# Seven products in the first pass of each MLP, the turned order in every pass, and pads between SBUF tiles

## The chip, the cores and the metric

The kernel runs on one core of a Trainium2 chip. The metric is the device time of one execution in microseconds (us); the median of three runs counts. TensorE (PE) multiplies matrices out of SBUF into the eight banks of PSUM, and its weight loads (PEld) run beside it. VectorE (DVE) and ScalarE (ACT) do element by element work, GpSimd (POOL) a few fills, and SyncE (SP) issues the DMAs that bring weights from HBM.

## The reference, cut to what matters

Two decoder layers over 256 positions with a width of 2048 in float32. The first mixes with a gated short convolution, the second with latent attention; each ends with an MLP, and every sub-layer with a layer norm of the residual.

```python
def sq_relu_mlp(x, w1, w2):
    return jnp.square(jax.nn.relu(x @ w1)) @ w2      # 2048 -> 8192 -> 2048

def reference(...):
    for layer in range(DEPTH):                        # DEPTH = 2
        ...
        h = layer_norm(ALPHA * h + mix, ln_g[layer, 0], ln_b[layer, 0])
        h = layer_norm(ALPHA * h + sq_relu_mlp(h, mlp_w1[layer], mlp_w2[layer]),
                       ln_g[layer, 1], ln_b[layer, 1])
    return h
```

## The kernel before

**Split operands.** The matmuls take operands rounded from float32 (type fp32r). Every operand is split into a high part (a cast on ScalarE, L121) and a low part (a subtraction on VectorE, L122), and a product is high x high + high x low + low x high.

**The weight stream.** All weights pass through one list, `stream`, in blocks of 128 x 1024. `take` hands out the next block and calls `prepare` for blocks up to five ahead: SyncE loads a raw block (five buffers, tag raw), ScalarE and VectorE split it into tiles hi and lo (eight buffers each). An entry of the list with two blocks becomes a pair (below). The order in which each engine finally runs its instructions is made by a scheduler from the order in which they are written, the priorities being that order; so work that waits for nothing may stand earlier on VectorE or ScalarE than it does in the text.

**The MLP** (`mlp`, called twice) walks over the 8192 hidden columns in NQ = 8 passes of QC = 8 blocks of 128. A pass has two halves:

- *Up.* Eight units, one for each hidden block. In pass 0 they are done by `mm_wide` on the input before its norm (258 columns: 256 positions and two columns for the norm's gain and offset), with x in the tiles of tags a1 and a2. From pass 1 on they are done by `products`: for each of 16 blocks k one matmul `high` with 512 columns (high and low part of x beside each other, L199) and one `low` with 256 (L203), 256 matmuls in a pass, x (`xhl`) in tag b. With `turned` set, unit 0 does low before high at k = TURNED = 2 once; before, this is so in pass 1 alone. Units put their sums into banks 0 and 1 in turn. `hidden` evacuates a unit, squares it and splits it into h (tag c).
- *Down.* h times the rows of w2, into four output blocks n of 512 columns for two halves t of the positions. `dot` does the three matmuls of a split product, 512 columns each (L283 to L285). Here h (128 columns) is loaded as the stationary operand, and the weights stream.

`down` does one output block in the plain way: 8 x 2 products, 48 matmuls. The passes in FAST (1 to 6) use Strassen-Winograd products instead: two blocks of h, two halves of the positions and two output blocks form a 2 x 2 by 2 x 2 product of blocks, which takes seven `dot`s in place of eight (`fast_products`, FACTORS). For this `prepare` builds from a pair of raw blocks the sums T1 to T4 (L154, L157, L160), and `hidden` builds S1 to S4 from h (L662 to L665) into `forms` (tag a2). The seven sums stay in seven banks and are added to `acc` (tag a1) or to `sums` by `keep` (L588; in pass 1 four of them are copied, L586). `fold`, in the last pass, adds `sums` into `acc`. In `down_pairs` the first two output blocks take four such units (84 matmuls); the last two follow MIXED = "ppsp": three quarters plain, the third quarter by seven products.

In pass 0 and pass 7 all four output blocks are plain: 192 matmuls. In pass 0 `put` copies a finished block to `acc` on ScalarE (L573) and then writes two calls of `normal` (L466 to L471), which compute the normed x for pass 1. In the second MLP passes 1 to 4 also add the turned residual (`extra`). In the first MLP, `begin` prepares the next norm (L397), written in the last pass.

**SBUF.** Pools are laid one behind another, and in a pool each tag gets its place when it is first used, as large as its largest tile: before, in pool act, xres, a1, a2, b, c, then S, Q, mu0 and ab; after act come raws, whl (hi, lo), tmp, small, and then the pool of the MLP (sums, fp, sf, t4).

Of the kernel before, what the change touches and what calls it, by code (L numbers as in the profile page):

```python
# [16 lines left out]
P = 128  # L17
W = 256 + 2
T = 256
# [16 lines left out]
BW = D // NB  # L36
FAST = range(1, NQ - 1)
MIXED = "ppsp"
FIRST = (0, 1, 2, 4, 6, 8, 12, 16)
HEAD = 4  # L40
GROUP = 3
# [10 lines left out]
def trunk(ctx: ExitStack, tc: tile.TileContext, xT, vecs, w_first, w_in, w_out, w_kv, w_q, w_uk, w_uv,  # L52
# [22 lines left out]
    def mlp_stream(l):  # L75
        out = []
        for q in range(NQ):
            out += halves(w1[l, q * QC:(q + 1) * QC])
            if q not in FAST:
                out += halves(w2[l, q])  # L80
                continue
            out += [(w2f[l, q, j, 0], w2f[l, q, j, 1]) for j in range(QC // 2)]
            for j, kind in enumerate(MIXED):
                if kind == "s":
                    out.append((w2g[l, q, j, 0], w2g[l, q, j, 1]))
                else:
                    out += halves(w2[l, q, 3, j]) + halves(w2[l, q, 2, j])
        return out
# [96 lines left out]
    def psum(name, bank=None):  # L185

        bank = Banks.next() if bank is None else bank
        return (pmm if bank < 4 else Banks.more).tile([P, 512], F32, tag=f"mm{bank}", name=name)
# [89 lines left out]
            yield ps  # L278


    def dot(ps, w, x, first, last):

        nc.tensor.matmul(ps, x[0], w[0], start=first, stop=False)  # L283
        nc.tensor.matmul(ps, x[0], w[1], start=False, stop=False)  # L284
        nc.tensor.matmul(ps, x[1], w[0], start=False, stop=last)  # L285

    def held(x, t):

        return [x[:, o + t * P:o + (t + 1) * P] for o in (0, T)]
# [2 lines left out]

        return [v[:, 4 * kk:4 * kk + 4, :].rearrange("p a c -> p (a c)") for v in w]

    def down(x, put, n):

        ps = [psum("ps_d") for _ in range(2)]
        for j in range(len(x) // 2):
            w, = take(1)
            for kk in range(2):  # L300
                k = 2 * j + kk
                for t in range(2):
                    dot(ps[t], wide_rows(w, kk), held(x[k], t), k == 0, k == len(x) - 1)
        for t in range(2):
            put(n, t, ps[t])
# [11 lines left out]
                put(n, t, ps)  # L317

    OWN, KEPT = ("1", "5", "7", "6"), (2, 3, 4, 5, 6, 7, 0)


    FACTORS = (("3", "S4", "22"), ("1", "11", "11"), ("5", "S1", "T1"), ("7", "S3", "T3"),
# [175 lines left out]
    banks = Banks.open("first")  # L498


    xres = act.tile([P, NC, T], F32, tag="xres", name="xres")
# [51 lines left out]
    def mlp(idx, ln, blocks, fast, begin=None, extra=None):  # L553
# [17 lines left out]
        def put(n, t, ps):  # L571
            if q == 0:
                nc.scalar.copy(block(n, t), ps)  # L573
                for _ in range(2):
# [6 lines left out]
        def keep(p, g, ps):  # L581

            at = sums[:, OWN.index(p), g, :] if p in OWN else \
                block(*{"2": (2 * g, 0), "3": (2 * g + 1, 0), "4": (2 * g, 1), "22": (2 * g + 1, 1)}[p])
            if q == 1 and p in OWN:
                nc.scalar.copy(at, ps)  # L586
            else:
                nc.vector.tensor_tensor(at, at, ps, ALU.add)  # L588

        def down_pairs(h, forms):  # L590

            n = QC // 2
            ps = {p: psum(f"ps_f{p}", bank) for (p, _, _), bank in zip(FACTORS, KEPT)}
            for j in range(n):
                fast_products(ps, h, forms, j, ps if j == 0 else (), ps if j == n - 1 else ())
            for p in ps:
                keep(p, 0, ps[p])
            ps = {p: psum("ps_d", bank) for p, bank in zip(("22", "3", "2", "4"), (1, *KEPT))}
# [32 lines left out]
        for q in range(NQ):  # L631
            ht = act.tile([P, QC, 2 * T], F32R, tag="c", name=f"h{idx}_{q}")
            h = [ht[:, k, :] for k in range(QC)]
            forms = None
# [4 lines left out]
            def pair_tile(m):  # L639

                if m % 2 == 0:
                    pool = (act, "ab") if m % 4 else (fast, "fp")
                    t = pool[0].tile([P, 2 * T], F32, tag=pool[1], name="fp")
                    pair.append(t.rearrange("p (i t) -> p i t", i=2))
                return pair[-1]

            def hidden(m, ps, evac, *func):
                both = pair_tile(m) if forms is not None else None
                f = both[:, m % 2, :] if forms is not None else tmp.tile([P, T], F32, tag="fh", name="fh", bufs=3)
# [4 lines left out]
                if forms is None:  # L654
                    put_split(h[m], f)
                elif m % 2:
                    at = ht[:, m - 1:m + 1, :]
                    split(at[:, :, :T], at[:, :, T:], both)
                    (a11, a21), (a12, a22) = ((both[:, i, :P], both[:, i, P:]) for i in range(2))
                    sf = fast.tile([P, 4, P], F32, tag="sf", name="sf")  # L660
                    s1, s2, s3, s4 = (sf[:, i, :] for i in range(4))
                    nc.vector.tensor_tensor(s1, a21, a22, ALU.add)  # L662
                    nc.vector.tensor_tensor(s3, a21, a11, ALU.subtract)
                    nc.vector.tensor_tensor(s2, s1, a11, ALU.subtract)
                    nc.vector.tensor_tensor(s4, a12, s2, ALU.subtract)  # L665
                    split(forms[:, m // 2, 0, :], forms[:, m // 2, 1, :], sf.rearrange("p i c -> p (i c)"))

            if q == 0:
                for m in range(QC):
                    if m < GROUP:  # L670
                        if m == 0:
                            ws = ln.ws if ln.ws else group_of(GROUP)
                            if not ln.ws:
                                mm_wide(ws, ln.xd)
                            ln.finish()
                        ps = ws[m][1]
                    else:
                        ws = [(take(), psum("ps_w"))]
                        mm_wide(ws, ln.xd)
                        ps = ws[0][1]  # L680
                    hidden(m, ps, ln.weighted, AF.Relu)
                    if m > 0:
                        normal()
                if begin:
                    begin(range(1))
                acc = act.tile([P, 2, D], F32, tag="a1", name=f"acc{idx}")
            else:
                folds = fold()
                for m, ps in enumerate(products(QC, xhl, TURNED if q == 1 else None, (0, 1))):
                    hidden(m, ps, whole)  # L690
                    if q == NQ - 1:
                        next(folds)
                        if begin:
                            begin(range(max(2 * m, 1), 2 * m + 2))

            if q == NQ - 1:
                blocks(block, put, h)
                return
            if q in FAST:
                down_pairs(h, forms)  # L700
            else:
                for n in range(NB):
                    down(h, put, n)

    def to_wide(block, put, h):

# [408 lines left out]
```

## Time and profile before

| what | value |
|---|---|
| three runs | 2034.58, 2035.73, 2036.16 us; median 2035.73 |
| profiled execution | 2035.76 us |
| its span, first to last instruction | 2034.0 us |
| granted TensorE clock | 1.000 over the whole span |
| VectorE busy | 1686.9 us, 83% |
| ScalarE busy | 1198.7 us, 59% |
| read from HBM | 381.25 MB, 188 GB/s over the span |
| splits of plain blocks (L121, L122) | 710 of each, 1050 and 1220 ns |
| plain down products (ps_d, L283 to L285) | 556 of each line, 391 ns busy |
| up products of passes 1 to 7 (ps_u) | 1792 high, 396 ns; 1792 low, 280 ns |

A matmul's busy time runs from the first column in to the last result out, so that of one overlaps that of the next; what it costs in a row of matmuls is the step from its start to the next one's. Stretches are given in us from the start of the span: the first MLP's pass 0 begins at about 364 with the up units and at 411 with the down products, its pass 1 at 454.8; in the second MLP pass 0's down products begin at 1371.3 and pass 1 at 1414.9.

### The profile page before, as it was taken

How to read it: one execution, taken by the hardware profiler on the slowest of the kernel's cores; microseconds unless marked ns; L12 is line 12 of the kernel's file. 1: busy time of each engine (PE TensorE's matmuls, PEld its weight loads, DVE VectorE, ACT ScalarE, POOL GpSimd, SP SyncE). 2: the span in 40 equal slices, each digit the busy share in tenths (PEclk: the TensorE clock that was granted, in tenths of full speed). 3: DMA queues.
4: the chain of work that ended last, by engine and by line, in shares of the span. 5: the costliest groups of instructions: out<-in, count | busy, mean ns of one | idle time of the engine just before them, and what ended most of it. 6: DMA issues, size and time to landing. Idle time of an engine off the chain costs nothing.

```text
span 2034.0 us, 30032 instructions
## 1 busy us (share of the span) xinstructions
PE 2025.4 (100%) x11204; PEld 1756.3 (86%) x11204; DVE 1686.9 (83%) x2571; ACT 1198.7 (59%) x1829; POOL 2.3 (0%) x21
## 2 busy tenths in 40 slices
PE   9999999999999999999999999999999999999998
PEld 8888888988888888888889998898888888888886
DVE  7667677788898988989888988776889898898986
ACT  6444445676666565655656655566666656566561
POOL 0000000000000000000000000000000000000000
PEclk9999999999999999999999999999999999999999
DMA  8666666564746557465754534656474655746573
GB/s 309 200 188 187 188 193 189 177 196 127 265 147 216 187 177 250 150 222 165 254 171 160 180 118 145 187 179 194 131 244 145 227 193 161 255 150 214 181 237 121
DMA packets 106850, 385.31 MB, mean 189 GB/s; under 512 B 11856, under 2 KB 12752, under 8 KB 106448
## 3 DMA queue, kind: packets, MB, share of 16 engines
q1 hardware_dynamic: 106560, 383.27, 58.6%
q8 instruction: 88, 1.44, 0.3%
q14 instruction: 58, 0.48, 0.1%
q10 hardware_dynamic: 144, 0.13, 0.0%
HBM read 381.25 MB, written 2.10 MB: 188 GB/s over the span
## 4 chain that ended last, share of the span: by engine, by line
PE 93%; DVE 4%; DMA 1%; issue 1%; ACT 1%; DVEq 0%; ACTq 0%
PE ps_u L199 20%; PE ps_l L199 13%; PE ps_u L203 10%; PE ps_l L203 7%; PE ps_d L283 6%; PE ps_d L285 6%; PE ps_d L284 6%; PE ps_f L283 3%; PE ps_f L285 3%; PE ps_f L284 3%; PE ps_w L233 2%; PE ps_w L231 2%; PE ps_w L232 2%; DMA raw<-in_w_dram 1%; DVE lo L122 1%; PE ps_g L233 1%
## 5 line engine op out<-in xcount | busy, mean ns | idle before, releaser
L122 DVE TENSOR_TENSOR lo<-raw,hi 128x1024 fp32r<-128x1024 f32 x710 | 857.4, 1220 | 225.1 <-ACT hi L121 153.8
L121 ACT CAST hi<-raw 128x1024 fp32r<-128x1024 f32 x710 | 741.6, 1050 | 396.8 <-DMA raw<-in_w_dram 117.1
L199 PE MATMUL ps_u<-xhl,hi 128*128 128x512 f32 x1792 | 629.6, 396 | 1.9 <-DVE sums L588 1.9
L203 PE MATMUL ps_u<-xhl,lo 128*128 128x256 f32 x1792 | 502.0, 280 | 0.0
L199 PEld LDWEIGHTS ps_u<-xhl,hi 128*128 128x128 f32 x1792 | 336.1, 188 | 83.7 <-ACT hi L121 3.0
L203 PEld LDWEIGHTS ps_u<-xhl,lo 128*128 128x128 f32 x1792 | 338.4, 189 | 0.6
L199 PE MATMUL ps_l<-xhl_a,hi 128*128 128x512 f32 x704 | 244.1, 393 | 0.0
L283 PE MATMUL ps_d<-hi,h 128*128 128x512 f32 x556 | 217.5, 391 | 0.2 <-DVE sums L588 0.2
L285 PE MATMUL ps_d<-hi,h 128*128 128x512 f32 x556 | 216.6, 390 | 0.0
L284 PE MATMUL ps_d<-lo,h 128*128 128x512 f32 x556 | 216.6, 390 | 0.0
L203 PE MATMUL ps_l<-xhl_a,lo 128*128 128x256 f32 x704 | 195.4, 279 | 0.0
L199 PEld LDWEIGHTS ps_l<-xhl_a,hi 128*128 128x128 f32 x704 | 132.1, 188 | 29.8
L203 PEld LDWEIGHTS ps_l<-xhl_a,lo 128*128 128x128 f32 x704 | 131.9, 188 | 0.2
L121 ACT CAST hi_t<-raw_t 128x1024 fp32r<-128x1024 f32 x60 | 63.0, 1050 | 108.8 <-DVE raw_t L154 93.3
L283 PEld LDWEIGHTS ps_d<-hi,h 128*128 128x128 f32 x556 | 104.4, 188 | 22.6 <-DVE sums L588 0.7
L285 PEld LDWEIGHTS ps_d<-hi,h 128*128 128x128 f32 x556 | 104.4, 188 | 22.1
L284 PEld LDWEIGHTS ps_d<-lo,h 128*128 128x128 f32 x556 | 104.4, 188 | 21.7
L652 ACT ACTIVATE fp<-fp 128x256 f32<-128x256 f32 x96 | 40.0, 417 | 81.5 <-DVE fp L338 80.7
L199 PE MATMUL ps_l<-z,hi 128*128 128x512 f32 x240 | 82.4, 391 | 0.0
L154 DVE TENSOR_TENSOR raw_t<-raw,raw 128x1024 f32<-128x1024 f32 x60 | 73.1, 1219 | 7.4 <-DMA raw<-in_w2f_dram 7.3
L122 DVE TENSOR_TENSOR lo_t<-raw_t,hi_t 128x1024 fp32r<-128x1024 f32 x60 | 73.2, 1220 | 1.3
L233 PE MATMUL ps_w<-xd,hi 128*128 128x258 f32 x256 | 72.9, 285 | 0.0
(270 smaller groups left out, 3359.9 us busy)
## 6 DMA issues: line engine op xcount, KB each, us to landing
raw<-in_w_dram SPq DMA_DIRECT2D x392, 512.0 KB, 4.5
raw<-in_w2f_dram SPq DMA_DIRECT2D x96, 512.0 KB, 3.7
raw<-in_w_in_dram SPq DMA_DIRECT2D x88, 512.0 KB, 4.3
raw<-in_w_out_dram SPq DMA_DIRECT2D x32, 512.0 KB, 4.2
raw<-in_w_o_dram SPq DMA_DIRECT2D x32, 512.0 KB, 4.0
raw<-in_w2g_dram SPq DMA_DIRECT2D x24, 512.0 KB, 5.0
raw<-in_w_kv_dram SPq DMA_DIRECT2D x10, 512.0 KB, 3.6
raw<-in_w_q_dram SPq DMA_DIRECT2D x8, 512.0 KB, 4.2
```

The costliest lines, as they stand in the source:

```text
L121: nc.scalar.copy(hi, src)
L122: nc.vector.tensor_tensor(lo, src, hi.bitcast(F32), ALU.subtract)
L154: nc.vector.tensor_tensor(t.rearrange(two, a=2), b12.unsqueeze(1).to_broadcast([P, 2, BW]), r1.rearrange(two, a=2), ALU.subtract)
L199: nc.tensor.matmul(ps, w[blk // 8][0][:, blk % 8, :], x, start=first, stop=False)
L203: nc.tensor.matmul(ps[:, :T], w[blk // 8][1][:, blk % 8, :], x[:, :T], start=False, stop=last)
L231: nc.tensor.matmul(ps[:, :W], hi, x[k][:, :W], start=k == 0, stop=False)
L232: nc.tensor.matmul(ps[:, :W], lo, x[k][:, :W], start=False, stop=False)
L233: nc.tensor.matmul(ps[:, :W], hi, x[k][:, W:], start=False, stop=k == NC - 1)
L283: nc.tensor.matmul(ps, x[0], w[0], start=first, stop=False)
L284: nc.tensor.matmul(ps, x[0], w[1], start=False, stop=False)
L285: nc.tensor.matmul(ps, x[1], w[0], start=False, stop=last)
L652: nc.scalar.activation(f, f, AF.Relu)
```

## The change

1. **Pads.** xres and the tags c, b, a1 and a2 get their places at the start, with tiles pad0 to pad2 between them and a last one in the pool small, and the tiles that matmuls read (h, xhl, forms, hi, lo, t4) then all begin at one place modulo 512 bytes. The scratch for POOL's DMAs is halved to 2048 bytes.
2. **Seven products in pass 0.** Its output blocks 2 and 3 are done first, plain; blocks 0 and 1 follow by `first_pair`, with the raw blocks as pairs. h of two blocks is kept together in float32 in `sums[:, 0:2]` and split two blocks at a time; the sums S1 to S4 of all four pairs are written behind the last up unit (`form`), when tag a2 is free. All seven results are copied by ScalarE. One block of `acc` is cleared by POOL, and `put` writes three calls of `normal`. In pass 1 the first pair's results are now all added by VectorE.
3. **Banks and order.** In the second pair the four own sums go to banks 0, 5, 6, 7 (before 5, 6, 7, 0), and the other four are added as soon as their block is done.
4. **The turn** stands in every pass from 1 to 7, and one product of the second pair (EVEN) does its middle matmul in two halves of 256 columns.

```diff
+EVEN = (QC - 1, "22")
...
+    xres = act.tile([P, NC, T], F32, tag="xres", name="xres")
+    for tag, columns in (("c", 4096), ("b", 8256), ("pad0", 64), ("a1", 4128), ("pad1", 96), ("a2", 4128), ("pad2", 96)):
+        act.tile([P, columns], F32, tag=tag, name=f"at_{tag}")
+    small.tile([P, 32], F32, tag="pad", name="at_pad", bufs=1)
...
-            if q not in FAST:
+            if q == NQ - 1:
                 out += halves(w2[l, q])
                 continue
+            if q == 0:
+                out += halves(w2[l, q, 2:])
             out += [(w2f[l, q, j, 0], w2f[l, q, j, 1]) for j in range(QC // 2)]
-            for j, kind in enumerate(MIXED):
+            for j, kind in enumerate(MIXED if q else ""):
...
-    def dot(ps, w, x, first, last):
+    def dot(ps, w, x, first, last, two=False):
         nc.tensor.matmul(ps, x[0], w[0], start=first, stop=False)
-        nc.tensor.matmul(ps, x[0], w[1], start=False, stop=False)
+        for at in (slice(0, T), slice(T, 2 * T)) if two else (slice(None),):
+            nc.tensor.matmul(ps[:, at], x[0], w[1][:, at], start=False, stop=False)
         nc.tensor.matmul(ps, x[1], w[0], start=False, stop=last)
...
-            if q == 1 and p in OWN:
+            if q == 0 or q == g == 1 and p in OWN:
                 nc.scalar.copy(at, ps)
...
-                        ps.update({p: psum(f"ps_f{p}", bank) for p, bank in zip(OWN, KEPT[3:])})
+                        ps.update({p: psum(f"ps_f{p}", bank) for p, bank in zip(OWN, OWN_BANKS)})
...
-                            dot(ps[p], wide_rows(w, kk), held(h[k], t), k == 0, k == QC - 1)
+                            dot(ps[p], wide_rows(w, kk), held(h[k], t), k == 0, k == QC - 1, (k, p) == EVEN)
+                    if j == n - 1:
+                        for _, p in two:
+                            keep(p, 1, ps[p])
...
-            for p in ("3", "2", "4", "22"):
-                keep(p, 1, ps[p])
...
+            def form(j):
+                (a11, a21), (a12, a22) = ((pair[j][:, i, :P], pair[j][:, i, P:]) for i in range(2))
+                sf = fast.tile([P, 4, P], F32, tag="sf", name="sf")
+                s1, s2, s3, s4 = (sf[:, i, :] for i in range(4))
+                nc.vector.tensor_tensor(s1, a21, a22, ALU.add)
+                nc.vector.tensor_tensor(s3, a21, a11, ALU.subtract)
+                nc.vector.tensor_tensor(s2, s1, a11, ALU.subtract)
+                nc.vector.tensor_tensor(s4, a12, s2, ALU.subtract)
+                split(forms[:, j, 0, :], forms[:, j, 1, :], sf.rearrange("p i c -> p (i c)"))
...
                 acc = act.tile([P, 2, D], F32, tag="a1", name=f"acc{idx}")
+                forms = act.tile([P, QC // 2, 2, 4 * P], F32R, tag="a2", name=f"forms{idx}_{q}")
+                nc.gpsimd.memset(block(1, 1), 0.0)
+                for j in range(QC // 2):
+                    form(j)
...
-                for m, ps in enumerate(products(QC, xhl, TURNED if q == 1 else None, (0, 1))):
+                for m, ps in enumerate(products(QC, xhl, TURNED, (0, 1))):
...
-            if q in FAST:
-                down_pairs(h, forms)
+            if q == 0:
+                down(h, put, 2, (2, 3))
+                down(h, put, 3, (1, 7))
+                first_pair(h, forms, (0, 2, 3, 4, 5, 6, 7))
             else:
-                for n in range(NB):
-                    down(h, put, n)
+                first_pair(h, forms, KEPT)
+                second_pair(h, forms)
...
-    nc = _bacc.Bacc("TRN2", target_bir_lowering=False, num_devices=1, dynamic_dma_scratch_size=4096)
+    nc = _bacc.Bacc("TRN2", target_bir_lowering=False, num_devices=1, dynamic_dma_scratch_size=2048)
```

`first_pair` and `second_pair` are the two halves of `down_pairs`.

More of the change, by code (lines that the diff above doesn't have):

```diff
@@ L293, in wide_rows, with down @@
         return [v[:, 4 * kk:4 * kk + 4, :].rearrange("p a c -> p (a c)") for v in w]
-    def down(x, put, n):
-        ps = [psum("ps_d") for _ in range(2)]
+    def down(x, put, n, banks=(None, None)):
+        ps = [psum("ps_d", bank) for bank in banks]
         for j in range(len(x) // 2):
@@ L573, in put @@
                 nc.scalar.copy(block(n, t), ps)
-                for _ in range(2):
+                for _ in range(3):
                     normal()
@@ L588, in keep, with first_pair @@
                 nc.vector.tensor_tensor(at, at, ps, ALU.add)
-        def down_pairs(h, forms):
+        def first_pair(h, forms, banks):
             n = QC // 2
-            ps = {p: psum(f"ps_f{p}", bank) for (p, _, _), bank in zip(FACTORS, KEPT)}
+            ps = {p: psum(f"ps_f{p}", bank) for (p, _, _), bank in zip(FACTORS, banks)}
             for j in range(n):
@@ L597, in down_pairs, with second_pair @@
                 keep(p, 0, ps[p])
+        def second_pair(h, forms):
+            n = QC // 2
             ps = {p: psum("ps_d", bank) for p, bank in zip(("22", "3", "2", "4"), (1, *KEPT))}
@@ L633, in mlp @@
             h = [ht[:, k, :] for k in range(QC)]
-            forms = None
+            firsts, forms = sums[:, 0:2].rearrange("p i g c -> p (i g) c"), None
             if q in FAST:
@@ L641, in pair_tile @@
                 if m % 2 == 0:
-                    pool = (act, "ab") if m % 4 else (fast, "fp")
-                    t = pool[0].tile([P, 2 * T], F32, tag=pool[1], name="fp")
+                    if q == 0:
+                        t = firsts[:, m // 2]
+                    else:
+                        pool = (act, "ab") if m % 4 else (fast, "fp")
+                        t = pool[0].tile([P, 2 * T], F32, tag=pool[1], name="fp")
                     pair.append(t.rearrange("p (i t) -> p i t", i=2))
                 return pair[-1]
+            def form(j):
[7 more added lines that the diff above has]
+                split(forms[:, j, 0, :], forms[:, j, 1, :], sf.rearrange("p i c -> p (i c)"))
             def hidden(m, ps, evac, *func):
-                both = pair_tile(m) if forms is not None else None
-                f = both[:, m % 2, :] if forms is not None else tmp.tile([P, T], F32, tag="fh", name="fh", bufs=3)
+                both = pair_tile(m) if q < NQ - 1 else None
+                f = both[:, m % 2, :] if both is not None else tmp.tile([P, T], F32, tag="fh", name="fh", bufs=3)
                 evac(ps, f, *func)
@@ L653, in hidden @@
                 nc.scalar.activation(f, f, AF.Square)
-                if forms is None:
+                if both is None:
                     put_split(h[m], f)
@@ L658, in hidden @@
                     split(at[:, :, :T], at[:, :, T:], both)
[L659 to L666, printed above, removed]
+                    if q:
+                        form(m // 2)
             if q == 0:
```

3 lines of the change are left out of this document (2 added, 1 removed).

## The prediction

> **What bounds the kernel now.** I read the page first, then the busy time by stretch, then single matmuls in the timeline, then the waits, and last VectorE's own timeline around the first pass of each MLP. The profiled execution took 2035.76 us with a span of 2034.0; the runs shown have a median of 2035.73, so the sum below is made against 2035.76 and stands for the median too. A change of this kernel is told from none at about 0.2%, 4.1 us.
>
> ```profile
> PE 2025.4 (100%) x11204; PEld 1756.3 (86%) x11204; DVE 1686.9 (83%) x2571; ACT 1198.7 (59%) x1829; POOL 2.3 (0%) x21
> ```
>
> PE is never idle, so time goes down only by fewer matmuls or by a shorter step from one start to the next. Its busy share can't show that step; counts over stretches can.
>
> ```profile
> 411.10:454.80 43.70, 43.70 (x194) 36.15 (x193) 35.90 (x67) 31.93 (x50) 0.00 (x0) 1.00 0.63 198
> 454.80:499.20 44.40, 44.40 (x258) 39.13 (x257) 33.68 (x51) 27.82 (x46) 0.00 (x0) 1.00 0.46 134
> 499.20:518.70 19.50, 19.50 (x87) 15.81 (x86) 18.07 (x24) 13.02 (x19) 0.00 (x0) 1.00 0.57 190
> 539.90:585.20 45.30, 45.30 (x258) 39.29 (x258) 38.79 (x58) 27.73 (x45) 0.00 (x0) 1.00 0.54 171
> 1371.30:1414.90 43.60, 43.60 (x195) 36.08 (x194) 31.10 (x51) 31.88 (x49) 0.00 (x0) 1.00 0.66 197
> ```
>
> Columns: stretch, length, busy time of PE, PEld, DVE, ACT and POOL with counts (a few at the edges belong to neighbours), clock, DMA. The first and last are pass 0's 192 plain down matmuls: 43.60/192 = 227.1 ns each. The third is the 84 matmuls of one seven-product pair: 19.5/84 = 232.1 ns, though all have 512 columns. The second and fourth are the same 256 up matmuls, 0.9 us apart. The timeline shows why (start, length): the first three lines are a slow pass, the last three a quick one.
>
> ```profile
> 550.17 0.40 PE L199 MATMUL ps_u<-xhl,hi 128*128 128x512 f32 x1
> 550.41 0.28 PE L203 MATMUL ps_u<-xhl,lo 128*128 128x256 f32 x1
> 550.53 0.40 PE L199 MATMUL ps_u<-xhl,hi 128*128 128x512 f32 x1
> ...
> 460.02 0.39 PE L199 MATMUL ps_u<-xhl,hi 128*128 128x512 f32 x1
> 460.25 0.28 PE L203 MATMUL ps_u<-xhl,lo 128*128 128x256 f32 x1
> 460.37 0.39 PE L199 MATMUL ps_u<-xhl,hi 128*128 128x512 f32 x1
> ```
>
> A slow pair takes 0.36 here (353.3 ns over the pass: wide steps of 233, 241 and 236 in turn), a quick pair 0.35 (230 + 117 = 347). Over a whole pass that is 176.6 against 173.4 ns a matmul, 0.82 us in 256. Of the 14 up passes nine are slow: all from pass 2 on in the first MLP; 2, 5 and 7 in the second. The state is chosen at the entry and then holds.
>
> **Fewer products.** Each first pass has 96 plain matmuls left (21.8 us) and 84 in place of 96. At 227.1 ns these take 19.1: 2.7 saved per MLP, 5.4 in two (2.3 and 4.7 at 232.1).
>
> **The pads.** Offsets follow from the tile sizes: a1 and a2 need 16,512 bytes, 128 over a multiple of 512, b 33,024, 256 over; the small pool 896. With the weights at 0 modulo 512, h and a1 lie at 0, forms (a2) at 128, xhl (b) at 256, T4 at 384. After, all are at 0. The row nearest: plain down matmuls, both operands at 0, step 227.1; the seven products alternate stationary operands at 0 and 128, and step 232.1, slowest just after a switch (241) and 227 between two of one h block. I take the gap for the price of switching. The 12 quick passes have 84 + 21 such matmuls: 12 x 105 x 5.0 ns = 6.3 us. Bounds: 0 and, with every switch also delaying its neighbour in the mixed pair, 7.
>
> The Trainium skill says otherwise: in "TensorE: Matmul & The Clock Gate", section "Back-to-back issue gap", a warm step is columns/2.4 plus 2.5 ns, 216 for 512, with no term for an address. The trace's 227.1 and 232.1 agree with neither the figure nor the missing term; by that rule the pads are worth 0, and the time would be that of the second rival.
>
> **The turn in every pass.** Both pass 1 entries, which have it already, come out quick; the others enter as chance has it. I let all nine slow passes become quick: 9 x 0.82 = 7.4. The alike stream ps_l from oT (416 matmuls at 176.4, in tag b) should profit from the pads: 416 x 3.0 ns = 1.2. Together 8.6. Bounds: 10.4 lost (below) to 9.3 gained. No faster state is expected: uniform streams with one offset step 227 (512 columns) and 120 (256, ps_q at 1126 us), together the quick pair's 347. The added turns cost some 20 ns each and the split EVEN matmul 2 x 120 - 227 = 13 ns, twelve times each: 0.4.
>
> **The waits on old sums.** In the second MLP passes 2 to 5 lose time at their end:
>
> ```profile
> PE ps_u L199 <- DVE sums L588: 1.9, 3, 1.0
> PE ps_d L283 <- DVE sums L588: 0.2, 1, 0.2
> ```
>
> Step by step in the timeline these cost 0.15 + 0.34 + 0.40 + 0.87 + 1.11 = 2.9 with the weight load behind them. The next up product needs bank 0, which the fourth addition ("6") frees; after, the first ("1") does, three steps of 0.6 = 1.8 us earlier, more than the longest wait. Late next is bank 1, wanted 5.5 us later, whose "22" is now added first, before the last block ends. I take 2.5.
>
> **VectorE in the first pass** is the price. A plain tile costs it one 128x1024 subtraction, 1.14 us from start to start (two in 2.35 at 1448.38). A pair of raw blocks costs 4 of those and three of 128x512 at 0.6: 6.4 in place of 2.3. Four: 16.3 more. The sums S1 to S4 add 4 x (4 x 0.2 + 0.6) = 5.6, all after the up products, since a2 is still held. So 21.9 more per MLP. DMAs stay: 8 raw blocks of 512 KB before and after.
>
> What hides it? VectorE's timeline:
>
> ```profile
> 435.33 1.21 DVE L122 TENSOR_TENSOR lo<-raw,hi 128x1024 fp32r<-128x1024 f32 x1
> 436.46 1.08 DVE L397 SCALAR_TENSOR_TENSOR xres<-xres,mu 128x256 f32<-128x256 f32 x3
> ...
> 442.53 1.23 DVE L122 TENSOR_TENSOR lo<-raw,hi 128x1024 fp32r<-128x1024 f32 x1 [1.49 <-ACT hi L121]
> ```
>
> ```profile
> 1390.79 0.41 DVE L471 TENSOR_TENSOR xhl<-xres,xhl 128x256 fp32r<-128x256 f32 x1
> 1391.96 1.22 DVE L122 TENSOR_TENSOR lo<-raw,hi 128x1024 fp32r<-128x1024 f32 x1 [0.75 <-ACT hi L121]
> ```
>
> It works without a pause until 441.0 and 1391.2, that is 30.0 and 19.9 us after the down products start; from then on it keeps seven weight tiles ahead of PE (counted: subtractions ended less tiles used) and idles. In the second MLP it has by then tiles 1 to 14; after, 8 of these are plain and the last six (6.8 us) turn into unit 0 (6.4), with 5.6 of sums added: unit 0 at 25, units 1 to 3 at 31.4, 37.8 and 44.2. PE needs a unit's last operand (T4) 18 matmuls, 4.1 us, after it begins it: 25.9 for unit 0, then 4.8 apart. Late: 0.7 + 1.6 + 1.6, and 0.4 for the first tile of pass 1: 4.3. In the first MLP ten replaced tiles (11.4) lie before 441.0: unit 0 and 5.0 of unit 1 at 35.6, unit 1 at 37.0 for 30.7; then 1.6, 1.6 and 0.4: 9.9. There 5.4 us are next-norm rows (L397) that nobody needs before pass 7; behind the units, 4.5 is left. I take the middle, 7.2. Together 11.5 us. Bounds: 0 (late normals go behind the units) and 21.9 per MLP. ACT gets 5.9 more for casts (0.95 for 128x1024, 0.52 for 128x512 between starts) and 2.1 for sums on 31.9 busy of 41, full too; its seven bank copies stand before the casts of pass 1, 0.6 each, in time for bank 0, whose product ends 4.1 early. In pass 1 four more additions on VectorE, 2.4 in the room of 19.5 against 18.1: 0.5. POOL's clearing of one block (0.5, as L744's) is due 60 us later: nothing.
>
> **Sum.** -5.4 - 6.3 - 8.6 - 2.5 + 0.4 + 11.5 + 0.5 = -10.4: 2035.8 - 10.4 = 2025.4, with VectorE's price between 4 and 18 a range of 2018 to 2032.
>
> **Rivals.** *VectorE's queue is ordered better* and the first pass doesn't wait: -21.9 gives 2013.9. For it: normals and L397 rows can go late; against: VectorE and ACT both are full. *Offsets don't matter*: 4.7 + 7.4 (the turn alone) + 2.5 less 12.4 is -2.2: 2033.6. For it: z and xhl, off the weights' offset, run quick; against: h against forms in one pass. The Trainium skill's rule cited above is this rival. *One offset locks the slow pair everywhere*, the other side: the five quick passes lose 4.1, ps_l on the opening's x 704 pairs x 6.5 ns = 4.6, on z 1.7: 10.4. With 5.4 + 6.3 + 2.5 gained and 12.4 paid this is +8.6: 2044.4. It is slower as soon as over 1.8 us are lost so, three of the five passes. For it: what chooses the state is not in the profile, and the slow one occurs only where moving operands share one offset throughout; against: ps_d and ps_q, all at one offset, show no such beat.
>
> **Chances.** Forecast 0.45, no wait 0.18, offsets without effect 0.18, slow everywhere 0.14; 0.05 for VectorE's price at 26, about 2040. Under 2031.7 lie 0.42 + 0.18 + 0.06 = 0.66 (faster); above 2039.8 lie 0.14 + 0.03 = 0.17; the rest, 0.17, is no change. The range 2011 to 2039 leaves out the slow case and the ends.
>
> **What would show it.** Up passes at 44.4 in all 14; 84 products in 19.1; ps_u no longer waiting for sums; PE idle on L283 to L285 in pass 0 with hi or lo as releaser, some 12 us in all, and none elsewhere. I am wrong if the wide steps still read 241, or if the two first passes wait over 20 us together.

## The result and the profile after

The changed kernel is slower: 2041.34 us (median of 20 runs, 2037.38 to 2045.04) against 2036.30 for the kernel before (20 runs, 2033.37 to 2039.69), a ratio of 1.0025 with an interval of 1.0019 to 1.0032. Forecast were 2025.4 us and a range that ended at 2039. The profiled execution took 2039.68 us with a span of 2037.8, 3.8 us more than before. What follows explains these 3.8 us of span; the medians lie 5.0 apart, and a part of the rest is in the first point of the last section.

The page's rows of engines, PE's first (busy time, share, instructions), after:

```profile
PE 2016.4 (99%) x11192; PEld 1749.0 (86%) x11192; DVE 1731.1 (85%) x2651; ACT 1211.6 (59%) x1843; POOL 3.3 (0%) x23
```

PE is busy 9.0 us less in a span that is 3.8 us longer: its own work did shrink, and about 12.8 us of idle time came in. The chain that ended last says the same. Its shares by engine, before and then after:

```profile
PE 93%; DVE 4%; DMA 1%; issue 1%; ACT 1%; DVEq 0%; ACTq 0%
```

```profile
PE 68%; DVE 19%; DMA 6%; issue 4%; ACT 3%; SPq 0%; DVEq 0%; ACTq 0%
```

Before, the chain runs through PE nearly all the time. After, a quarter of it has moved to VectorE, the DMAs and ScalarE: a loop of these engines decides together with PE. The stretches that answer to the five shown before (length, then busy time of PE, PEld, VectorE, ScalarE and POOL with counts, clock, DMA):

```profile
411.90:458.30 46.40, 43.47 (x183) 33.18 (x181) 46.40 (x86) 34.52 (x54) 0.00 (x0) 1.00 0.36 103
458.30:503.40 45.10, 45.10 (x256) 39.15 (x256) 43.53 (x66) 33.94 (x53) 0.00 (x0) 1.00 0.65 223
503.40:522.50 19.10, 19.10 (x86) 15.79 (x85) 17.52 (x24) 13.03 (x17) 0.00 (x0) 1.00 0.64 200
543.60:588.00 44.40, 44.40 (x257) 39.11 (x257) 38.46 (x56) 29.36 (x46) 0.00 (x0) 1.00 0.57 184
1372.80:1418.20 45.40, 42.42 (x183) 33.31 (x181) 44.90 (x80) 33.79 (x54) 0.00 (x0) 1.00 0.34 104
```

Pass 0 (first and last line) got longer, 43.7 to 46.4 and 43.6 to 45.4; VectorE is busy for nearly its whole length. The 84 pair products (third line) fell from 19.5 to 19.1, as forecast. The up half of pass 2 (fourth) fell from 45.3 to 44.4, as forecast; that of pass 1 (second) rose from 44.4 to 45.1, which the forecast did not have. PE's waits (us in total, times, longest):

```profile
PE ps_d L292 <- DVE sums L598: 7.4, 9, 1.3
PE ps_f L292 <- ACT hi_t L130: 4.8, 4, 1.7
```

The second row is pass 0, and was expected. The first is a wait for old sums. Such waits were to shrink nearly to nothing, and have grown: before, all of them together were 2.1 us in these rows.

I added up the span in pieces, before against after. A pass has an up half and a down half. From pass 1 to 6 a down half without a wait takes 40.75 us before and 40.20 after (0.89 more in the four passes that also add the residual); as "waits" I count what the down halves take beyond that. Waits inside an up half stay in the row of the up halves.

| piece | change, us |
|---|---|
| two first passes, 43.7 to 46.4 and 43.6 to 45.4 | +4.5 |
| twelve times 84 pair products, 19.48 to 19.08 | -4.8 |
| twelve times the rest of the down half (mixed quarter and the plain products beside it), 0.15 less each | -1.8 |
| fourteen up halves: nine slow before (0.82 each); after, two (pass 1), and 0.3 and 1.0 more in passes 4 and 5 of the second MLP | -4.8 |
| stream on z (480 matmuls), 173.4 to 176.6 ns | +1.5 |
| the other opening streams (743 and 665 matmuls), 0.3 and 0.5 ns less | -0.6 |
| waits in the down halves of passes 1 to 6, 0.0 + 3.1 to 5.5 + 7.7 | +10.0 |
| the rest of the span | -0.2 |
| sum | +3.8, of 3.8 |

The new waits in the down halves are the largest entry. One of them, in pass 4 of the first MLP, as the chain shows it (start, length, what):

```profile
772.31 1.15 DVE lo L131
773.46 0.02 issue
773.47 5.48 DMA raw<-in_w_dram
778.95 0.02 issue
778.98 1.06 ACT hi L130
780.04 0.02 issue
780.06 0.17 DVE lo L131
780.23 0.97 issue
781.20 0.69 DVE sums L598
781.89 0.04 issue
781.94 0.50 PE ps_d L292
```

Read from the end: a plain product of the second pair starts at 781.94, when the addition of "1" has freed its bank. That addition stands in VectorE's order behind the subtraction of a weight block (L131), which waits for the block's cast on ScalarE, which waits for its DMA (5.48 us), which waits for the raw buffer that an earlier subtraction has freed at 773.46. This is a ring: VectorE, DMA, ScalarE, VectorE, closed by the five raw buffers. VectorE's own timeline at that place, before and then after (start, length, line, operation; in brackets its idle time and what ended it):

```profile
776.39 1.23 DVE L122 TENSOR_TENSOR lo<-raw,hi 128x1024 fp32r<-128x1024 f32 x1 [0.25 <-ACT hi L121]
777.53 1.87 DVE L588 TENSOR_TENSOR sums<-sums,ps_f 128x512 f32<-128x512 f32 x3
```

```profile
776.93 2.35 DVE L131 TENSOR_TENSOR lo<-raw,hi 128x1024 fp32r<-128x1024 f32 x2
780.06 1.22 DVE L131 TENSOR_TENSOR lo<-raw,hi 128x1024 fp32r<-128x1024 f32 x1 [0.78 <-ACT hi L130]
781.20 1.88 DVE L598 TENSOR_TENSOR sums<-sums,ps_f 128x512 f32<-128x512 f32 x3
```

The first pair's products end at 776.56 before and at 777.74 after. So the additions begin 0.97 us behind that end before, 3.46 after. The bank of "1" is due 12 matmuls behind it, 2.74 us, and an addition takes 0.69: it must begin by 2.0. Over passes 2 to 6 of the first MLP the additions begin 0.67 to 1.21 behind the pair's end before, and 2.2 to 3.5 after. **The addition that the ring feeds ended about 1 us ahead of its due time at this place, and now ends 0.2 to 1.4 us behind it**, because PE's pass without waits became 1.4 us shorter (85.96 to 84.59: 0.82 in the up half, 0.40 in the pair, 0.15 in the rest) and the ring did not. A lead of 1 us is used up once; from then on PE goes at the ring's pace. VectorE is idle in that very loop (0.25 and 0.78 in the brackets): its busy share, 83 or 85%, doesn't show that it is late.

### The profile page after: what moved, and what is told of

It is laid out like the page before. It is cut to its first block, busy times and chain, and to the rows that moved or that the text cites. A ratio compares the mean times of both kernels' runs of the same rounds, so it can differ in the third digit from the quotient of the medians.

```text
span 2037.8 us, 30076 instructions
## 1 busy us (share of the span) xinstructions
PE 2016.4 (99%) x11192; PEld 1749.0 (86%) x11192; DVE 1731.1 (85%) x2651; ACT 1211.6 (59%) x1843; POOL 3.3 (0%) x23
## 4 chain that ended last, share of the span: by engine, by line
PE 68%; DVE 19%; DMA 6%; issue 4%; ACT 3%; SPq 0%; DVEq 0%; ACTq 0%
PE ps_l L208 13%; PE ps_u L208 12%; PE ps_l L212 7%; DVE lo L131 6%; PE ps_u L212 6%; DMA raw<-in_w_dram 4%; PE ps_d L292 4%; PE ps_d L295 4%; PE ps_d L294 4%; ACT hi L130 2%; DVE lo_t L131 2%; DVE raw_t L163 2%; PE ps_f L294 1%; PE ps_f L295 1%; PE ps_f L292 1%
## 5 line engine op out<-in xcount | busy, mean ns | idle before, releaser
L131 DVE TENSOR_TENSOR lo<-raw,hi 128x1024 fp32r<-128x1024 f32 x710 | 858.1, 1221 | 185.1 <-ACT hi L130 113.6
L292 PE MATMUL ps_d<-hi,h 128*128 128x512 f32 x492 | 193.9, 394 | 7.5 <-DVE sums L598 7.4
L295 PE MATMUL ps_d<-hi,h 128*128 128x512 f32 x492 | 191.9, 390 | 0.0
L294 PE MATMUL ps_d<-lo,h 128*128 128x512 f32 (+1 forms) x504 | 191.8, 384 | 0.0
L130 ACT CAST hi_t<-raw_t 128x1024 fp32r<-128x1024 f32 x68 | 71.4, 1050 | 112.7 <-DVE raw_t L163 108.8
L292 PEld LDWEIGHTS ps_d<-hi,h 128*128 128x128 f32 x492 | 92.4, 188 | 30.6 <-DVE sums L598 12.0
L294 PEld LDWEIGHTS ps_d<-lo,h 128*128 128x128 f32 x504 | 94.7, 188 | 19.2
L295 PEld LDWEIGHTS ps_d<-hi,h 128*128 128x128 f32 x492 | 92.4, 188 | 19.1
L163 DVE TENSOR_TENSOR raw_t<-raw,raw 128x1024 f32<-128x1024 f32 x68 | 82.9, 1220 | 9.0 <-DMA raw<-in_w2f_dram 8.9
L131 DVE TENSOR_TENSOR lo_t<-raw_t,hi_t 128x1024 fp32r<-128x1024 f32 x68 | 82.9, 1220 | 1.4 <-ACT hi_t L130 0.3
```

The source lines that it names most:

```text
L130: nc.scalar.copy(hi, src)
L131: nc.vector.tensor_tensor(lo, src, hi.bitcast(F32), ALU.subtract)
L163: nc.vector.tensor_tensor(t.rearrange(two, a=2), b12.unsqueeze(1).to_broadcast([P, 2, BW]), r1.rearrange(two, a=2), ALU.subtract)
L294: nc.tensor.matmul(ps[:, at], x[0], w[1][:, at], start=False, stop=False)
```

## The experiments

Three theories went into the first runs. *The ring*: PE's gain is waited for again, since the loop with five raw buffers needs some 85.8 us for the blocks of a pass, however fast PE is. *The lost lead*: the first pass with seven products leaves VectorE behind, and it never catches up. *The banks*: the new order of part 3 puts the additions in the wrong place. All edits below are made to the kernel after, unless the kernel before is named; ratios are to the kernel before.

### First pass plain again

```diff
-            if q == 0:
-                out += halves(w2[l, q, 2:])
...
-                down(h, put, 2, (2, 3))
-                down(h, put, 3, (1, 7))
-                first_pair(h, forms, (0, 2, 3, 4, 5, 6, 7))
+                for n in range(NB):
+                    down(h, put, n)
```

> The changed kernel with a plain first pass (part 2 undone, the rest kept). Ring theory: from pass 2 on a pass can't be shorter than some 85.8 us, which is what the ring VectorE - raw DMA - ScalarE - VectorE takes for it, so the 1.2 us that the quicker matmuls save in each pass are waited for again at L292 on the sums of L598. Then pass 0 is back at 43.6 us of down products without a wait, pass 1 enters quick (44.4 us), and later passes still wait on sums, 5 to 9 us in all instead of 10; time 2029 to 2035 against 2036 before. Lost-lead theory (the waits only come from pass 0 having used up the lead): no waits on sums in passes 2 to 6, time 2018 to 2023. Theory of banks and order (the additions stand later because of part 3): waits on sums stay at 10 us, time 2031 or more.

Measured: 2036.32 us (2032.95 to 2038.35), ratio 0.9992 (0.9983 to 1.0000), span 2034.5. PE's waits:

```profile
PE ps_d L290 <- DVE sums L596: 9.1, 10, 1.6
```

With pass 0 as before, the waits on sums stay, 9.1 us in ten places against 7.4 in nine, so the lost lead falls. The time is a little above what the ring theory gave (2029 to 2035), since there are more waits than after. Pass 1's up half is quick again, 44.39 in both MLPs, so what made it slow came with the pass 0 ahead of it.

### Old banks and order

```diff
-                        ps.update({p: psum(f"ps_f{p}", bank) for p, bank in zip(OWN, OWN_BANKS)})
+                        ps.update({p: psum(f"ps_f{p}", bank) for p, bank in zip(OWN, KEPT[3:])})
...
-                    if j == n - 1:
-                        for _, p in two:
-                            keep(p, 1, ps[p])
...
+            for p in ("3", "2", "4", "22"):
+                keep(p, 1, ps[p])
```

> The changed kernel with the banks and the order of the additions of before (part 3 undone). Theory of banks and order: the waits on the second pair's start fall from 10 us to the 0.4 that before had; time 6 to 9 us under the changed kernel. Ring theory: the waits stay at the same place and size, and the end of a pass waits for bank 0 besides, so the time is the changed kernel's or up to 4 us above it.

Measured: 2042.82 us (2038.85 to 2048.99), ratio 1.0023 (1.0014 to 1.0032). The profiled execution is the longest one, with a span of 2047.2.

```profile
PE ps_d L292 <- DVE sums L598: 5.1, 8, 0.9
...
PE ps_u L208 <- DVE sums L598: 3.2, 5, 1.1
```

The sum of the two rows, 8.3, is a little more than the one row had. The wait moves partly to the start of the next up half, and nothing is gained: the order of the additions is not the cause. But the state of the up halves shows what that order is good for. Nine of them begin behind such a wait here (their first step is 305 to 310 ns), and of these four are quick (44.5) and five slow (45.3), though all have the turn; pass 6 of the first MLP is slow (45.2) too, with a first step of 233 ns. After, none begins behind a wait, and all of passes 2 to 7 begin quick.

### Six raw buffers, and its control

To make room, one buffer of the tags sq and ropea goes and POOL's scratch falls to 512 bytes. The control does this alone, with five raw buffers.

```diff
-RAW, WA = 5, 8
+RAW, WA = 6, 8
...
-    nc = _bacc.Bacc("TRN2", target_bir_lowering=False, num_devices=1, dynamic_dma_scratch_size=2048)
+    nc = _bacc.Bacc("TRN2", target_bir_lowering=False, num_devices=1, dynamic_dma_scratch_size=512)
```

> The changed kernel with six raw buffers in place of five (room from a single buffer for tag sq and a DMA scratch of 512 bytes). Ring theory: a raw block is asked for one block earlier, some 4 us of slack in the ring, so the waits on sums in passes 1 to 6 fall from 10 us to under 3 and the time by 6 to 10 us, to 2031 to 2035. Theory of banks and order, and lost lead: VectorE has the same work in the same order, so the waits stay and the time changes by less than 2 us.

> The changed kernel with the single buffer for tag sq and the DMA scratch of 512 bytes that made room for the sixth raw buffer, but with five raw buffers. Ring theory: nothing of the gain of the six buffers is here; waits on sums about 10 us, time within 2 us of the changed kernel's 2041. Rival (the room, a moved address or the single sq buffer made the gain): waits under 3 us and time near 2026.

Measured: six buffers 2026.00 us (2025.23 to 2027.08), ratio 0.9942 (0.9929 to 0.9955); the control 2042.27 (2038.87 to 2045.05), ratio 1.0026 (1.0015 to 1.0037). One more buffer of 512 KB is worth 16 us between these two, more than the 6 to 10 that were expected. PE's longest waits with six, and VectorE at the place shown above:

```profile
PE ps_f L292 <- ACT hi_t L130: 4.8, 4, 1.6
PE offset L1038 <- DVE udiag L1036: 1.2, 1, 1.2
```

```profile
770.46 4.80 DVE L131 TENSOR_TENSOR lo<-raw,hi 128x1024 fp32r<-128x1024 f32 x4
...
776.29 1.23 DVE L131 TENSOR_TENSOR lo<-raw,hi 128x1024 fp32r<-128x1024 f32 x1 [0.44 <-ACT hi L130]
777.44 0.68 DVE L598 TENSOR_TENSOR acc<-acc,ps_f 128x512 f32<-128x512 f32 x1
778.03 1.88 DVE L598 TENSOR_TENSOR sums<-sums,ps_f 128x512 f32<-128x512 f32 x3
```

No row of ps_d for sums is left; the additions to sums begin 1.45 us behind the pair's end (776.58). The waits in the down halves fall from 5.5 and 7.7 to 0.5 and 0.0, and a pass takes 84.6 to 85.2 us (85.5 in the four passes that also add the residual), where it took 85.0 to 87.5. The waits of pass 0 are untouched (4.8 in the first row): these aren't the ring's. The span falls by 14.5: 12.7 of waits and 2.2 in up halves that are quick for their whole length now, with 0.4 lost elsewhere. These two runs are what the ring theory stands on.

### Pads alone, on the kernel before

```diff
+    xres = act.tile([P, NC, T], F32, tag="xres", name="xres")
+    for tag, columns in (("c", 4096), ("b", 8256), ("pad0", 64), ("a1", 4128), ("pad1", 96), ("a2", 4128), ("pad2", 96)):
+        act.tile([P, columns], F32, tag=tag, name=f"at_{tag}")
+    small.tile([P, 32], F32, tag="pad", name="at_pad", bufs=1)
```

> The kernel before with the pads alone. All theories: the 84 products of each quick pass take 19.1 us in place of 19.5, the up passes are quick or slow by a state that the pads may change. Ring theory: of 6.3 us saved in twelve passes only 1 to 3 show in the time, the rest is waited for. Without a ring: 6 us less, apart from what the up passes' state does (0.82 us for each pass).

POOL's scratch is halved as well. Measured: 2037.03 us (2033.11 to 2037.97), ratio 0.9992 (0.9983 to 1.0000), span 2035.3.

```profile
PE ps_d L288 <- DVE sums L591: 4.1, 7, 0.9
PE ps_u L204 <- DVE sums L591: 2.7, 5, 1.0
```

The pair products take 19.1 everywhere, 4.8 us less in sum, and none of it shows in the time: the waits in the down halves rise from 0.0 and 3.1 to 3.1 and 7.5, and z takes 176.6 in place of 173.4 ns (1.5). It is the forecast's error in small: the step of PE got its gain, and the ring took it back.

The ring's own time can be read here. Passes 2 to 6 of the first MLP take 85.7 us each on the mean in this kernel, in the kernel after and in that with the plain first pass. Without waits PE would need 85.0 here and 84.6 in the other two, so the pace is not PE's. Before, PE needed 85.96 and did not wait in these passes.

### Plain first pass and six raw buffers; then six raw buffers on the kernel before

The first takes the edits of the first and third experiment together, the second that of the third on the kernel before; this line is in both:

```diff
-RAW, WA = 5, 8
+RAW, WA = 6, 8
```

> The changed kernel with a plain first pass and six raw buffers (and their room). Ring theory with the price of the first pass as seen (9.5 us of waits against 5.4 us saved in two MLPs): 4 us under the six buffers with seven products, that is 2021 to 2023, and passes 1 to 6 of 84.6 us (85.5 with the turned residual). If the plain first pass gives nothing once the ring is loose: 2025 to 2027.

> The kernel before with six raw buffers (and their room). Ring theory: before, PE's own 86.0 us a pass hid the ring, and only the second MLP's 3 to 4 us of waits on sums can go: 2032 to 2035. If six buffers are a gain of their own, whatever PE's pace: 2026 or less.

The first: 2021.32 us (2019.93 to 2023.64), ratio 0.9925 (0.9913 to 0.9938), against 2026.00 and 0.9942 with seven products in pass 0: these cost 4.7 us net in the medians. The spans, 2020.6 and 2023.3, differ by 2.7 only, since this profiled execution still waits in the second MLP, 3.1 us in the down halves:

```profile
PE ps_d L290 <- DVE acc L596: 1.0, 3, 0.5
```

So with six buffers the waits are not gone in every execution. All fourteen up halves take 44.39.

The second changes nothing: 2034.92 us (2034.54 to 2035.80), ratio 0.9992 (0.9983 to 1.0001). Its waits:

```profile
PE offset L1011 <- DVE udiag L1009: 1.2, 1, 1.2
PE warm L353 <- DVE col L355: 1.1, 1, 1.1
PE ps_g L199 <- ACT hi L121: 0.8, 1, 0.8
```

None of the longest is for sums; the waits in the down halves of the second MLP fell from 3.1 to nothing; but there passes 3, 4 and 6 now take 45.21 in their up half, where they took 44.45 before. So for the kernel before the ring was hardly a bound; without the quicker PE the buffer is worth 1.1 us of span.

### Which part makes the up halves quick

Three kernels, all with six raw buffers: the one above with the turn in pass 1 alone; the same with the turn everywhere but without EVEN; and the kernel before with turn and EVEN, but neither pads nor new banks.

```diff
-                for m, ps in enumerate(products(QC, xhl, TURNED, (0, 1))):
+                for m, ps in enumerate(products(QC, xhl, TURNED if q == 1 else None, (0, 1))):
```

```diff
-                            dot(ps[p], wide_rows(w, kk), held(h[k], t), k == 0, k == QC - 1, (k, p) == EVEN)
+                            dot(ps[p], wide_rows(w, kk), held(h[k], t), k == 0, k == QC - 1)
```

```diff
-                for m, ps in enumerate(products(QC, xhl, TURNED if q == 1 else None, (0, 1))):
+                for m, ps in enumerate(products(QC, xhl, TURNED, (0, 1))):
...
+                            dot(ps[p], wide_rows(w, kk), held(h[k], t), k == 0, k == QC - 1, (k, p) == EVEN)
```

> The changed kernel with a plain first pass, six raw buffers, and the turn in pass 1 alone (pads, banks and EVEN kept). If the turn makes an up pass quick: passes 2 to 7 are at 45.2 us in most cases, up to 0.82 us lost in each of twelve, 2027 to 2032. If the pads make it quick: all at 44.4 and the time that of the kernel with the turn in every pass, 2021 to 2023.

> The changed kernel with a plain first pass and six raw buffers, without the split matmul (EVEN), so that a pass from 1 to 6 has 433 matmuls in place of 434. If the parity of the matmuls before an up pass decides whether the turn makes it quick: every other pass at 45.2 us, some six in all, 2025 to 2027. If only the turn counts: all passes at 44.4, 2020 to 2023.

> The kernel before with the turn in every pass, the split matmul and six raw buffers, without pads and with the old banks. Offsets theory: up passes quick by the turn alone (44.4), the 84 products of a quick pass still at 19.5 us, and the time some 6.3 us above the same with pads (2021.3) less 1.6 for the stage on z, which is quick without pads: 2025 to 2028. If offsets don't matter: 19.1 us for the products, 2020 to 2022.

Measured: without the turn 2029.30 us (2029.06 to 2030.18), 0.9963 (0.9949 to 0.9977); without EVEN 2019.87 (2019.66 to 2021.31), 0.9919 (0.9905 to 0.9932); without pads 2026.04 (2025.84 to 2026.61), 0.9948 (0.9935 to 0.9960). The up halves of passes 3 and 4 of the first MLP with the turn and then without:

```profile
625.00:669.40 44.40, 44.40 (x257) 39.12 (x256) 37.26 (x55) 27.13 (x44) 0.00 (x0) 1.00 0.56 174
709.60:754.00 44.40, 44.40 (x258) 39.13 (x257) 38.27 (x56) 28.15 (x45) 0.00 (x0) 1.00 0.56 181
```

```profile
625.80:671.00 45.20, 45.20 (x258) 39.18 (x257) 37.69 (x55) 27.31 (x44) 0.00 (x0) 1.00 0.55 172
711.20:756.40 45.20, 45.20 (x257) 39.23 (x256) 38.52 (x56) 27.43 (x45) 0.00 (x0) 1.00 0.58 178
```

Without the turn all twelve passes 2 to 7 are slow, pads or not; with it all are quick, pads or not (the kernel without pads has 44.39 in all fourteen). The turn does it, and twelve times 0.82 is 9.8 us; the medians differ by 8.0, and the kernel with the turn is the one whose profile still has 3.1 us of waits. The pads do nothing for the up halves. They are worth 0.60 us in a down half without a wait, 0.40 of it in the pair (19.48 without them, 19.08 with): 7.2 in twelve, less the 1.5 on z. EVEN does nothing that can be told in the time: the intervals of 0.9919 and 0.9925 overlap.

### What makes z slow

The turn one pair later, and tag b (which holds z) 256 bytes off the weights' offset:

```diff
-            for _ in range({TURNED - 1: 0, TURNED: 2}.get(g, 1)):
+            for _ in range({TURNED: 0, TURNED + 1: 2}.get(g, 1)):
```

```diff
-    for tag, columns in (("c", 4096), ("b", 8256), ("pad0", 64), ("a1", 4128), ("pad1", 96), ("a2", 4128), ("pad2", 96)):
+    for tag, columns in (("c", 4096), ("pad0", 64), ("b", 8256), ("a1", 4128), ("pad1", 96), ("a2", 4128), ("pad2", 96)):
```

> The changed kernel with a plain first pass and six raw buffers, and the turn of the lagged streams (conv in, z, oT) one matmul pair later, at its number 3 in place of 2. If the place of the turn sets these streams' state: the stage on z goes from 176.6 ns a matmul to 173.4 (1.6 us) or oT does (1.2 us), and the conv in stage may be lost (4.5 us): 2018 to 2026. If the offset sets it: all three as they are, 2020 to 2023.

> The kernel of the last round without the split matmul (plain first pass, six raw buffers, pads, turn, new banks), with pad0 ahead of tag b in place of behind it, so that z, xhl and oT lie 256 bytes off the weights' offset, as before the change, and h, forms and t4 at it. If the offset of the streamed operand sets the state of the stage on z: 173.4 ns a matmul there in place of 176.6, 1.6 us, and 2017.5 to 2019 with all else as it is. If it is not that offset (but the addresses of other tiles, or the code ahead): z stays at 176.6 and the time at 2020. The twelve turned up passes are expected at 44.4 either way, since they were with and without pads.

The first is made to the kernel with plain first pass and six raw buffers, the second to that without EVEN. Measured: 2022.87 us (2022.25 to 2024.68), 0.9933 (0.9918 to 0.9948), with z still at 176.6 ns and the opening's first stretch (743 matmuls) now at 177.2 in place of 173.9; and 2020.07 (2019.41 to 2021.01), 0.9915 (0.9901 to 0.9928), with z at 176.6 and all up halves at 44.39. So where the turn stands matters for one stretch, and the streamed operand's offset for none. z is slow in every run with the pads, also with the pads alone, and quick in the three kernels without them (before, with six raw buffers, and with turn and EVEN). So the pads' layout makes it slow; by which address stays open.

The quickest version by its median is the change without its second part and without EVEN, with a sixth raw buffer: 2019.87 us, 0.8% under the kernel before. It can't be told from the last one above (2020.07).

## Why the prediction was wrong

- **The waits on old sums** is the step that failed. It let the 2.9 us of waits shrink by 2.5, since bank 0 would be freed 1.8 us earlier. That is right for the wait it looked at (ps_u for sums is gone), and the bank of "1", wanted 12 matmuls behind the first pair, was never costed. The waits in the down halves grew by 10.0 us: 12.5 of the 14.2 between the forecast -10.4 and the measured +3.8. Behind it stands the premise that, as PE is never idle, a shorter step is a shorter time. PE was not idle because the ring, at 85.7 us a pass, was just faster than PE's 85.96. Then 1.4 us a pass were taken from PE alone, and in passes 2 to 6 of the first MLP the ring let only 0.3 of it through. VectorE's timeline around a pair's end would have warned: the additions ended (0.97 + 0.69) some 1.1 us before their bank was due, in a loop through a DMA. Neither of the forecast's two signs of being wrong came (wide steps of 241, over 20 us of waits in the first passes); both looked elsewhere.
- **The turn in every pass** was forecast at -8.6. Ten of the twelve passes 2 to 7 of the two MLPs went to 44.39; two of the second MLP began quick and became slow behind a wait in their middle (44.74 and 45.40). The step let pass 1, which had the turn already, stay quick, and after a pair of seven products it came out slow twice (45.1 and 45.2); with a plain pass 0 it is quick. So the up halves gave -4.8. The 1.2 us expected of oT were nothing (176.4 before and after), and z went slow, +1.5, for which the forecast's sum had no term; the rival in which one offset locks the slow pair everywhere had one, of 1.7. That rival's time (2044.4) is near the measured one, and the forecast's tail case with VectorE's price at 26 (about 2040) nearer still. Both are luck: ten of fourteen up halves are quick throughout, z is as slow with b off the common offset, and VectorE's price was 9.6.
- **The pads** were right: 232.1 to 227.2 ns (19.08/84), -4.8 and -1.8 against -6.3; between two kernels that both have EVEN it was 7.2, just over the forecast's bound of 7. The timeline shows the switches between h and forms without the wide step of 241 ns (start, length):

```profile
591.02 0.39 PE L294 MATMUL ps_f<-lo,h 128*128 128x512 f32 x1
591.24 0.39 PE L295 MATMUL ps_f<-hi,h 128*128 128x512 f32 x1
591.47 0.39 PE L292 MATMUL ps_f<-hi,forms 128*128 128x512 f32 x1
591.70 0.39 PE L294 MATMUL ps_f<-lo,forms 128*128 128x512 f32 x1
```

  Each step is 0.22 or 0.23, across the switch as within a block. The formula of the Trainium skill behind the second rival ("TensorE: Matmul & The Clock Gate", section "Back-to-back issue gap") has the columns alone in it, and the page gives it for an isolated matmul. In these rows of matmuls the same 512 columns take 232.1 or 227.2 ns in the two layouts, so that rival falls.
- **VectorE in the first pass** was right in kind and nearly in size: forecast 11.5 of waits against 5.4 saved; measured 5.2 + 4.4 = 9.6 beyond the usual steps, and +4.5 net for +6.1. That this part costs more than it saves was in the forecast, term by term.
- **Fewer products** came out as forecast: without those waits pass 0 takes 41.2 and 41.0 us, forecast 40.9. The 0.4 us for turns and EVEN and the 0.5 for the additions of pass 1 are too small to be told in the time.

## What to carry to other kernels

An engine that is busy 100% of the span hides how little the next bound lies behind it. Before a part of its work is shortened, look at one place of each pass how long ahead of its due time the neighbour's last instruction ends. A lead of 1 us there, as here, is used up once; what a pass can gain for good is its length less the time that the neighbour's own loop needs for it (85.96 - 85.7 here), and where that time isn't known, the gain isn't either. Look for loops through a DMA and a fixed number of buffers above all, since an engine in such a loop can be late while its busy share is far below 100%. One more buffer was worth 16 us here with the quicker PE and 1 us without, so the two have to be tried together.

## What the runs showed that was not expected

- PE's waits seem to cost it clock too. In two profiles with seven products in pass 0 the granted clock falls to 0.5 for 3.41 us right behind the waits of that pass (from 456.0 and 1421.9 with the old banks, from 1416.7 in the control with five raw buffers), and a matmul of 512 columns steps by 427 ns there; about 1.7 us are lost each time, by an estimate from half of 3.41. The profile of the kernel after has no such fall, but 13 of its 20 runs list a mean clock below 1.000 (median 2042.1 us, against 2039.9 in the other seven). Of the 64 runs of the kernel before that list a clock, two do, and of the 44 with six raw buffers, one. The forecast had no term for this; that the waits bring the fall is likely, but was not tested.
- A stream of alternating wide and narrow up products has two steps, 173.4 and 176.6 ns a matmul, and without a wait it keeps one for a whole pass. Swapping one pair of them at its entry makes it the quick one in every pass of the runs with six raw buffers that follows a plain or mixed half; behind the seven-product pair that ends pass 0 it does not (45.0 to 45.2 in seven of the eight such passes run). Why is open.
- A wait goes with a change of the state, in both directions. Before, passes 3, 4 and 6 of the second MLP were quick (44.45) without the turn, and became slow (45.21) when the sixth buffer took the waits away; pass 5 has a wait and is slow all the same. With the old banks five of nine passes behind a wait were slow in spite of the turn. After, passes 4 and 5 of the second MLP turn slow at their seventh and fifth unit, where a weight load waits 0.20 and 0.32 us; a wait of 0.30 at the third unit of pass 5 changes nothing. Which state follows a wait looks like chance; no run shows what decides it.
- Products with alternating stationary operands step by 232.1 ns in the layout before, in which the operands lie 0 and 128 bytes over a multiple of 512, and by 227.2 with the pads, in which all lie at 0. Only these two layouts of them were run, so that the offset modulo 512 is the cause, and not another property of the addresses, is likely but not shown. The offset of the streamed tile z changed neither its own step nor that of the up halves.
